# Windowed and dense attention in one encoder layer on one core: meta tokens' keys in a part of their own, and new places on the time line

## The chip, the cores and the metric

The kernel runs on one core of a Trainium2 chip. The metric is device time in microseconds (us), measured from outside. A core has a matrix engine (TensorE, PE in the profile; its weight loads are listed apart as PEld), a vector engine (VectorE, DVE), an activation engine (ScalarE, ACT), a general engine (GpSimd, POOL) and a queue engine that issues transfers (SyncE, SP). Each works through its own instructions in the order in which they stand, and waits on semaphores for the others.

## The reference

One layer, applied to two requests of 1024 tokens each (`g` below) with shared weights. Sixteen meta tokens stand ahead of every request; their rows are dropped from the output. All is float32.

```python
proj = h @ w_in                        # queries, keys, values, z of branches A and B; gates ga, gb
ya = window_attention(rotate(qa), rotate(ka), va, sink) * silu(za)
yb = dense_attention(axial_rope(rms_norm(qb)), axial_rope(rms_norm(kb)), vb) * silu(zb)
merged = sigmoid(ga) * (ya @ w_branch_a) + sigmoid(gb) * (yb @ w_branch_b)
h = layer_norm(ALPHA * h + merged @ w_out)
```

Branch A sees, for a block of 128 queries, the 16 meta keys and the blocks before, at and after its own (|i-j| <= 128), with a sink logit per head. Branch B sees all 16 + 1024 keys. Both have 8 query heads and 2 key-value heads of 64.

## The kernel before

**Precision.** A float32 product is made of three matmuls in the reduced type fp32r: each operand is split into a rounded part (`h`) and a rest (`l`), and the products hh, hl and lh are added in PSUM. So a projection of 128 tokens onto 512 columns is 8 x 3 matmuls of 512 columns. Scores take two matmuls (the query tiles `q1`, `q2` against packed keys), and a value product two (the scores' rounded part `ph` and rest `pl` against values whose rounded part and rest stand side by side).

**Stages.** Stage one (to about 290 us) projects keys and values of all 16 token blocks, and two of the four gates, and keeps keys and values in DRAM (`kd`, `vd`; those of the meta tokens in SBUF tile `mk` and in DRAM `vmd`). Then come branch A (2 requests x 8 blocks), branch B (the same), the other two gates, and a last stage with the branch projections, the output projection and the layer norm. Between A and B lies the handover: `weight_b` (line 840) loads the query and z weights of branch B in 16 pieces of 128 x 512; SP fetches each, ACT rounds it, DVE or POOL makes the rest.

**A unit.** `unit` (line 739) handles one block of 128 queries of one key-value head, four query heads at a time. There are 32 units in each branch. Its steps: `queries` transposes and splits the queries; `scores(h)` makes the scores of head h into one bank of PSUM for each key chunk, and DVE takes minima (in branch A with the mask added); `exps(h)` lets ACT write the exponentials into tiles `p`; `part(k)` takes some keys of all four heads, transposes them on PE (four transposes `st<-ident,p`), copies the result rounded to `ph` on ACT, and subtracts to get `pl` on DVE; `values(k)` adds two 512-wide matmuls, `o<-ph,v` and `o<-pl,v`, to the output bank. `gather`, `scale_z` and `gate` finish the unit.

**Parts.** The meta keys are laid among the others (`keys`, line 608), and `rows` (617) cuts the row of keys in equal parts: in branch A 400 keys into 4 parts of 100 (272 keys into 3 parts of 91, at the first and last block), in branch B 1040 keys into three chunks of 348, 348 and 344, and 9 parts of 116 (the last 112). A 128-row part without meta keys would match the token blocks; here a part takes rows of two blocks, and `chunk` (622) loads values by several transfers, the meta rows by one of them.

**What sets the order.** The functions do not issue instructions but record them. Each recorded step carries a key, a place on a time line (`at`, line 600, with the numbers of `AT`, `LN` and `BOOST`, lines 48 to 51). `Plan.issue` (line 238) then walks all engines in time with a price for every instruction, and at each step lets the engine that is free first take the ready instruction of the lowest key. What comes out is a fixed order for each engine, which the hardware follows. All instructions are recorded at line 279, so rows of the profile differ by tile names only.

Of the kernel before, what the change touches and what calls it, by code (L numbers as in the profile page):

```python
# [12 lines left out]
F32 = mybir.dt.float32  # L13
F32R = mybir.dt.float32r
# [8 lines left out]
P = 128  # L23
# [9 lines left out]
XF = 3  # L33
WF1 = 8
GSPLIT = 1
WB_STEP, WB_LEAD = 1.4, 2.5
DELAY = {
    "pe": {"pe": 0.0, "act": 0.2, "dve": 0.2, "pool": 0.22, "dma": 0.2},
# [3 lines left out]
}  # L42
TABLES = {AF.Exp: "exp", AF.Tanh: "exp", AF.Sigmoid: "sigmoid"}
TABLE_LOAD = 1.28
DMA_ISSUE, DMA_START, DMA_DONE = 0.475, 2.0, 1.8
PB = (7, 3, 3)
KB = 5
BC, BR = 348, 116
NB = 3
OFF = (3, 3)  # L50
ROPE_TAGS = (("rq1", 1), ("rq2", 1), ("rqo", 2))
WSUB = (0, 1, 1, 1)
BOOST = {"rotate": 12, "silu": 12, ("fillq", 0): 2.18, ("fillq", 1): 3.7, ("fillz", 0): -3.9, ("fillz", 1): 4.15, ("values", 0): -1.06, ("values", 1): -1.8, ("gather", 0): 0, ("gather", 1): 0, ("scale_z", 0): 0, ("gate", 0): 0}
LN, LN_LAST = (11.2, 17.85), 18
AT = ({"queries": 22, "scores": 8, "head": 0.7, "exps": 1.85, "part": 2.5},
      {"queries": 22.2, "scores": 6, "head": 4.25, "exps": 4.05, "part": 1.65})
ALPHA = 2.0 ** 0.25
SCALE = HD ** -0.5
NEG = -1e30
# [109 lines left out]
class Plan:  # L169
# [3 lines left out]
    def __init__(self, nc):  # L173
        self.ops, self.rings, self.key = [], {}, 0.0
        self.engines = [Engine(self, e, n) for e, n in
                        ((nc.tensor, "pe"), (nc.scalar, "act"), (nc.vector, "dve"), (nc.gpsimd, "pool"), (nc.sync, "dma"))]
        self.free = {e.id: 0.0 for e in self.engines}
        self.bus, self.tables = 0.0, None

    def tile(self, pool, shape, dtype, tag=None, name=None, bufs=1, space="sbuf"):  # L180
        name = name or tag
# [50 lines left out]
    @staticmethod  # L232
    def delay(d, op):
        if d.eng.id == "dma":
            return DMA_DONE
        return DELAY[d.eng.id][op.eng.id]

    def issue(self):
        done = []
        wait = {e: [] for e in self.free}  # L240
        ready = {e: [] for e in self.free}
        for i, op in enumerate(self.ops):
            op.num = (op.key, i)
            for d in op.deps:
                if d.end is None:
                    d.next.append(op)
                    op.left += 1
                else:
                    op.ready = max(op.ready, d.end + self.delay(d, op))
            if not op.left:  # L250
                heapq.heappush(wait[op.eng.id], (op.ready, op.num))
        for _ in self.ops:
            t, e = min((self.free[e] if ready[e] else max(self.free[e], wait[e][0][0]), e)
                       for e in self.free if ready[e] or wait[e])
            while wait[e] and wait[e][0][0] <= t:
                heapq.heappush(ready[e], heapq.heappop(wait[e])[1])
            op = self.ops[heapq.heappop(ready[e])[1]]
            if op.tables not in (None, self.tables):
                self.tables = op.tables
                t += TABLE_LOAD  # L260
            self.free[e] = op.end = t + op.cost
            if e == "dma":
                self.free[e] = t + DMA_ISSUE
                op.end = self.bus = max(self.bus, t + DMA_START) + op.cost
            for n in op.next:
                n.ready = max(n.ready, op.end + self.delay(op, n))
                n.left -= 1
                if not n.left:
                    heapq.heappush(wait[n.eng.id], (n.ready, n.num))
            done.append(op)  # L270
        for op in done:
# [7 lines left out]
            getattr(op.eng.real, op.name)(*map(real, op.a), **{k: real(v) for k, v in op.k.items()})  # L279
        self.ops = []  # L280


@with_exitstack
def encoder(ctx, tc, d, out):
# [332 lines left out]
    def rows(b, c):  # L617

        n = sum(n for *_, n in keys(b, c))
        return BR if b else -(-n // -(-n // P))  # L620

    def chunk(b, g, e, c):

        if (b, g, e, c) not in chunks:
            at_ = 0
            if e:
                t = kvp.tile([P, 4, NKV, P], F32R, tag="v", name="v", bufs=4)
                r = rows(b, c)
                for meta_, i, m in keys(b, c):
                    while m:  # L630
                        j, o = divmod(at_, r)
                        k, w = (m // r * r, m // r) if o == 0 and m >= r else (min(m, r - o), 1)
                        src = vmd[0:NM, b] if meta_ else vd[b][g]
                        dst = t[o:o + k // w, j:j + w].bitcast(F32)
                        dma(dst, src[i:i + k].rearrange("(w p) v e -> p w v e", w=w))
                        at_, i, m = at_ + k, i + k, m - k
# [10 lines left out]
        return chunks[b, g, e, c]  # L647

    def block_proj(b, g, t, blk, t0, ln):

# [88 lines left out]
    def unit(b, g, t, kvh, blk, t0, ln):  # L739


        cs = list(range(NB)) if b else [t]
        n = [sum(m for *_, m in keys(b, c)) for c in cs]
        r = rows(b, t if b == 0 else 0)
        np_ = [-(-m // r) for m in n]
        parts = [(i, j) for i, m in enumerate(np_) for j in range(m)]
        m0 = 0 if t > 0 else P
        heads = slice(kvh * G, (kvh + 1) * G)
        s = {"p": {}, "part": {}}
# [1 line left out]
        def scores(h):  # L751
# [11 lines left out]
            for i, sx in enumerate(s["sx", h]):  # L763
# [1 line left out]
                if b:  # L765
                    nc.vector.tensor_reduce(out=mn, in_=sx, op=ALU.min, axis=AX.X)
                else:
                    p = s["p"][h, 0] = wk.tile([P, 400], F32, tag=f"p{h if h < 3 else kvh}", name="p", bufs=PB[0])
# [11 lines left out]

        def exps(h):
            for i, sx in enumerate(s["sx", h]):
                if b:
                    s["p"][h, i] = wk.tile([P, 400], F32, tag=f"p{i}", name="p", bufs=PB[0])
                p = s["p"][h, i][:, 0:n[i]]
                act(p, sx if b else p, AF.Exp, scale=-1.0, bias=s["nb"][:, h:h + 1], accum_out=s["rs"][:, h, i:i + 1])

        def sinks():
# [7 lines left out]
                ptt(out=s["rs"][:, :, 0], in0=s["rs"][:, :, 0], in1=s["rs"][:, :, i], op=ALU.add)  # L796

        def part(k):
            i, j = parts[k]
            m = min(r, n[i] - j * r)  # L800
            st = bank("st", 2)[0:m]
            for h in range(G):
                nc.tensor.transpose(st[:, h * P:(h + 1) * P], s["p"][h, i][:, j * r:j * r + m], ident)
            ph = wk.tile([P, 512], F32R, tag="ph", name="ph", bufs=PB[1])[0:m]
            pl = wk.tile([P, 512], F32R, tag="pl", name="pl", bufs=PB[2])[0:m]
            s["part"][k] = ph, pl
            act(ph, st, AF.Copy)
            tt(out=pl, in0=st, in1=ph.bitcast(F32), op=ALU.subtract)

        def values(k):  # L810
            if k == 0:
                s["o"] = bank("o", 1)
            i, j = parts[k]
            m = min(r, n[i] - j * r)
            v = chunk(b, g, 1, cs[i])[0:m, j, kvh]
# [24 lines left out]
    def weight_b(i, t0):  # L840
# [15 lines left out]
        for k in range(KT):  # L856
            at(t0 + WB_STEP * k - WB_LEAD, lambda k=k: fetch(k))
            at(t0 + WB_STEP * k, lambda k=k: piece(k))

    clock, last = 0.0, LN[0]  # L860
    for b in range(2):
        for g in range(2):
            for t in range(NT):
# [172 lines left out]
```

## Time and profile before

| what | value |
|---|---|
| median of 3 runs | 1797.1 us (1795.17 to 1799.28) |
| the profiled execution | 1799.36 us |
| its span, first to last instruction | 1797.6 us |
| busy PE / DVE / ACT / POOL | 1767.0 / 1134.5 / 879.4 / 250.6 us |
| mean granted clock of TensorE | 0.994 |

The span is what the trace covers; the rest of the profiled execution's time lies around it. The profile gives for each group of instructions its tiles as out<-in, its shape (partitions x elements, of a matmul also weights as rows*columns), how often it ran, its busy time in us and the mean duration of one in ns, and then the engine's idle time ahead of it with what ended it. Recorded durations of neighbouring matmuls overlap, since they are pipelined. In the timeline the first number is the start from the beginning of the span, the second the duration; x4 merges four in a row.

### The profile page before, as it was taken

What the parts mean: (1) busy time and instruction counts of PE and PEld (TensorE: products, weight loads), DVE (VectorE), ACT (ScalarE), POOL (GpSimd) and SP (SyncE); (2) the same over time, 40 slices, a digit from 0 to 9 for tenths busy, and PEclk for the clock granted to TensorE, in tenths of its full rate; (3) what the DMA queues carried; (4) which work ended last, traced back from release to release, by engine and by line L of the source; (5) the groups of instructions that cost most, each with busy time, mean ns of one, the idle gap of its engine ahead of it and who ended that gap; (6) DMA issues with size and microseconds to landing.
All of it is one profiled execution on the core that took longest, in us unless ns stands there. A gap on an engine that the chain in (4) does not pass through costs nothing.

```text
span 1797.6 us, 26170 instructions
## 1 busy us (share of the span) xinstructions
PE 1767.0 (98%) x8906; PEld 1453.1 (81%) x8906; DVE 1134.5 (63%) x2900; ACT 879.4 (49%) x2257; POOL 250.6 (14%) x437
## 2 busy tenths in 40 slices
PE   7999999999999999999999999999999999999997
PEld 5787787888888878888888888877888788888886
DVE  6533334777677778888888888886300355555555
ACT  5322223666666677777777777788411310000000
POOL 2000002222221231011111111132000011111110
PEclk9999999999999999999999999999999999999999
DMA  9644445422322340100002000122654643333321
GB/s 326 222 159 143 161 148 161 152 92 91 109 92 91 116 140 32 56 30 34 30 34 77 30 33 30 47 92 68 249 161 152 212 160 117 118 115 115 110 78 48
DMA packets 111083, 199.09 MB, mean 111 GB/s; under 512 B 11796, under 2 KB 49876, under 8 KB 110948
## 3 DMA queue, kind: packets, MB, share of 16 engines
q1 hardware_dynamic: 110948, 197.40, 32.8%
q8 instruction: 71, 1.16, 0.3%
q14 instruction: 64, 0.52, 0.1%
HBM read 138.60 MB, written 58.75 MB: 110 GB/s over the span
## 4 chain that ended last, share of the span: by engine, by line
PE 93%; DVE 2%; DMA 2%; ACT 1%; issue 0%; POOL 0%; SPq 0%; DVEq 0%; ACTq 0%
PE st L279 32%; PE pj L279 26%; PE o L279 18%; PE sx L279 14%; PE tr L279 2%; DMA wf<-in_w_in_dram 0%; DVE mn L279 0%; ACT p L279 0%; DMA gsc<-sg 0%; POOL rope L279 0%; DMA rope<-in_rope_b_dram 0%; DMA wf<-in_wkv_dram 0%; DVE pl L279 0%; SPq L279 0%; DMA sg<-gsc 0%
## 5 line engine op out<-in xcount | busy, mean ns | idle before, releaser
L279 DVE TENSOR_TENSOR pl<-st,ph 116x512 fp32r<-116x512 f32 (+4 forms) x408 | 276.8, 684 | 51.4 <-ACT ph L279 46.1
L279 ACT ACTIVATE ph<-st 116x512 fp32r<-116x512 f32 (+4 forms) x408 | 242.9, 598 | 113.2 <-PE st L279 109.6
L279 PE MATMUL st<-ident,p 128*116 128x128 f32 (+4 forms) x1632 | 257.8, 273 | 3.3 <-ACT p L279 2.2
L279 PE MATMUL sx<-k,q 128*128 128x348 f32 (+3 forms) x1024 | 246.5, 341 | 2.6 <-ACT q L279 0.9
L279 PEld LDWEIGHTS st<-ident,p 128*116 128x116 f32 (+4 forms) x1632 | 198.9, 134 | 52.6 <-issue 7.1
L279 ACT ACTIVATE p<-sx,nb 128x348 f32<-128x348 f32 (+1 forms) x384 | 206.8, 549 | 59.4 <-DVE nb L279 58.7
L279 DVE TENSOR_REDUCE mn<-sx 128x1 f32<-128x348 f32 (+1 forms) x384 | 192.0, 513 | 45.4 <-PE sx L279 42.8
L279 PEld LDWEIGHTS sx<-k,q 128*128 128x128 f32 x1024 | 171.3, 190 | 27.0 <-ACT p L279 4.4
L279 PE MATMUL o<-ph,v 116*128 116x512 f32 (+4 forms) x408 | 176.8, 433 | 0.5 <-DVE yu L279 0.3
L279 DVE TENSOR_TENSOR xl<-xf,xh 128x512 fp32r<-128x512 f32 x64 | 58.2, 927 | 180.6 <-ACT xh L279 180.6
L279 PE MATMUL o<-pl,v 116*128 116x512 f32 (+4 forms) x408 | 164.9, 404 | 1.9 <-DVE pl L279 1.9
L279 ACT ACTIVATE xh<-xf 128x512 fp32r<-128x512 f32 x64 | 38.8, 627 | 258.6 <-PE sx L279 190.1
L279 POOL TENSOR_TENSOR sg<-sg 128x512 f32<-128x512 f32 x32 | 46.9, 1464 | 466.0 <-DVE sg L279 291.8
L279 PE MATMUL pj<-w0h,xh 128*128 128x512 f32 x272 | 111.5, 410 | 0.0
L279 PE MATMUL pj<-w1h,xh 128*128 128x512 f32 x264 | 110.4, 418 | 0.5 <-DVE rope_rq L279 0.5
L279 PE MATMUL pj<-w0h,xl 128*128 128x512 f32 x272 | 108.4, 398 | 0.0
L279 PE MATMUL pj<-w0l,xh 128*128 128x512 f32 x272 | 107.3, 395 | 0.0
L279 PE MATMUL pj<-w1l,xh 128*128 128x512 f32 x264 | 106.2, 402 | 0.0
L279 PE MATMUL pj<-w1h,xl 128*128 128x512 f32 x264 | 105.3, 399 | 0.0
L279 ACT ACTIVATE q<-tr 64x256 fp32r<-64x256 f32 x256 | 96.4, 376 | 16.6 <-PE tr L279 13.8
L279 PEld LDWEIGHTS o<-pl,v 116*128 116x128 f32 (+4 forms) x408 | 77.2, 189 | 20.3 <-DVE pl L279 11.5
L279 ACT ACTIVATE p<-p,nb 128x400 f32<-128x400 f32 (+1 forms) x128 | 75.8, 595 | 33.4 <-DVE nb L279 33.2
(198 smaller groups left out, 3775.0 us busy)
## 6 DMA issues: line engine op xcount, KB each, us to landing
xh<-xsc SPq DMA_DIRECT2D x48, 512.0 KB
xl<-xsc SPq DMA_DIRECT2D x48, 512.0 KB
wf<-in_w_in_dram SPq DMA_DIRECT2D x64, 256.0 KB
gsc<-sg SPq DMA_DIRECT2D x64, 256.0 KB
sg<-gsc SPq DMA_DIRECT2D x64, 256.0 KB
xf<-in_xt_dram SPq DMA_DIRECT2D x32, 256.0 KB
xsc<-xh SPq DMA_DIRECT2D x16, 512.0 KB
xsc<-xl SPq DMA_DIRECT2D x16, 512.0 KB
```

Source lines behind the costliest of these rows:

```text
L279: getattr(op.eng.real, op.name)(*map(real, op.a), **{k: real(v) for k, v in op.k.items()})
```

## The change

Meta keys get a part of their own, and all other keys are cut in parts of 128.

- Branch B's chunks are 384, 384 and 272 keys (the last with the 16 meta keys), with 3 + 3 + 2 parts; branch A has 3 parts (2 in the first and last block). That is one part fewer in each of the 64 units: 344 parts, for 408.
- `meta_near` copies the meta columns of the four heads' exponentials side by side on POOL (`pc`, 128 x 64). `meta_part` transposes them at once on PE, and writes the rounded part into rows 0 to 63 of a tile `pm` (ACT), the rest into rows 64 to 127 (DVE). `meta_out` adds four matmuls `o<-pm,vm`, one for each head, 128 columns wide, with weights `vm` that hold the meta values in that head's rows and zeros elsewhere.
- `vm` is made once for each branch: POOL clears it, and eight transfers of 16 rows fill it.
- The exponentials of the four heads share a tile, with four buffers (two for the third chunk of branch B) for seven of each head's or chunk's; value tiles have 3 slots for 4; weight pieces of the handover use three staging buffers for four.
- The planner assumes 0.9 for 1.8 us as the end of a transfer in stage one. The numbers of the time line are chosen anew (`BOOST`, `LN`, `LN_LAST`, `AT`, and the start of the second weight's load); of these the diff shows two lines.

```diff
-DMA_ISSUE, DMA_START, DMA_DONE = 0.475, 2.0, 1.8
-PB = (7, 3, 3)
+DMA_ISSUE, DMA_START, DMA_DONE = 0.475, 2.0, (0.9, 1.8)
+PB = (4, 2, 3, 3)
-BC, BR = 348, 116
+BC = 384
-AT = ({"queries": 22, "scores": 8, "head": 0.7, "exps": 1.85, "part": 2.5},
+AT = ({"queries": 21.23, "scores": 8, "head": 0.7, "exps": 3.19, "part": 2.0},
...
+    def meta_values(b):
+        t = vm[b] = wk.tile([P, NKV, G, P], F32R, tag="vm", name="vm", bufs=1)
+        nc.gpsimd.memset(t.rearrange("p v h e -> p (v h e)").bitcast(F32), 0.0)
+        for r in (0, 64):
+            for h in range(G):
+                dma(t[r + h * NM:r + (h + 1) * NM, :, h].bitcast(F32), vmd[0:NM, b])
...
         def part(k):
-            i, j = parts[k]
-            m = min(r, n[i] - j * r)
-            st = bank("st", 2)[0:m]
+            i, o = parts[k]
+            st = bank("st", 2)
             for h in range(G):
-                nc.tensor.transpose(st[:, h * P:(h + 1) * P], s["p"][h, i][:, j * r:j * r + m], ident)
+                nc.tensor.transpose(st[:, h * P:(h + 1) * P], s["p"][i][:, h, o:o + P], ident)
...
+        def meta_near():
+            pc = s["pc"] = wk.tile([P, G * NM], F32, tag="pc", name="pc", bufs=2)
+            nc.gpsimd.tensor_copy(pc.rearrange("p (h m) -> p h m", h=G), s["p"][mi][:, :, mo:mo + NM])
+        def meta_part():
+            st = bank("st", 2)
+            nc.tensor.transpose(st[0:64, 0:P], s["pc"], ident)
+            pm = s["pm"] = wk.tile([P, P], F32R, tag="pm", name="pm", bufs=2)
+            act(pm[up], st[0:64, 0:P], AF.Copy)
+            tt(out=pm[dn], in0=st[0:64, 0:P], in1=pm[up].bitcast(F32), op=ALU.subtract)
+        def meta_out():
+            for h in range(G):
+                mm(s["o"][:, h * P:(h + 1) * P], lhsT=vm[b][:, kvh, h], rhs=s["pm"], start=False, stop=False)
...
+        km = META_AT[b]
+        at(t0 + km * slot - T["part"] - 1.5, meta_near, ("part", b))
+        at(t0 + km * slot - T["part"] - 0.01, meta_part, ("part", b))
+        at(t0 + km * slot - 0.01, meta_out, ("values", b))
...
-            f[k] = stage() if k % 4 < 3 else wk.tile([P, 512], F32, tag="wf", name="wf", bufs=1)
+            f[k] = stage()
...
-                    weight_b(1, clock + 2 * ln - 6.53)
+                    weight_b(1, clock + 2 * ln - 8.21)
```

The order of PE in branch A, near the start of the second request. Before (`st<-ident,p` are the transposes of a part, `sx` scores, `o` value products, `tr` transposes of queries and gates, `pj` projections):

```order
L279 MATMUL st<-ident,p 90x128 x4
L279 MATMUL tr<-ident,zr 128x128 x2
L279 MATMUL st<-ident,p 100x128 x4
L279 MATMUL sx<-k,q_5375 128x400
L279 MATMUL sx<-k,q_5189 128x400
L279 MATMUL o<-ph,v 128x512
L279 MATMUL sx<-k,q_5375 128x400
L279 MATMUL sx<-k,q_5189 128x400
L279 MATMUL sx<-k,q_5375 128x400
L279 MATMUL sx<-k,q_5189 128x400
L279 MATMUL o<-pl,v 128x512
L279 MATMUL st<-ident,p 100x128 x4
```

And about the same stretch after, with the transpose of the meta columns (`pc`) and the four narrow matmuls:

```order
L279 MATMUL st<-ident,pc 64x128
L279 MATMUL st<-ident,p 128x128 x4
L279 MATMUL pj<-w0h,xh 128x512
L279 MATMUL pj<-w0l,xh 128x512
L279 MATMUL pj<-w0h,xl 128x512
L279 MATMUL pj<-w0h,xh 128x512
L279 MATMUL pj<-w0l,xh 128x512
L279 MATMUL pj<-w0h,xl 128x512
L279 MATMUL o<-pm,vm 128x128 x4
L279 MATMUL o<-ph,v 128x512
L279 MATMUL o<-pl,v 128x512
L279 MATMUL st<-ident,p 128x128 x4
```

Four transposes of 90, 91 or 100 columns have become four of 128; between the transpose of `pc` and the matmuls that use its split stand four transposes and six projection matmuls. In the handover this distance is once four transposes and three projection matmuls.

The order of POOL in branch B, two units, before (`q` is cleared for later queries, `rs` are the row sums, `zr` the scaled gate):

```order
L279 MEMSET q_9057 64x512
L279 TENSOR_TENSOR rs<-rs 128x4 x2
L279 TENSOR_TENSOR zr<-z,rs 128x256
L279 MEMSET q_9304 64x512
L279 TENSOR_TENSOR rs<-rs 128x4 x2
L279 TENSOR_TENSOR zr<-z,rs 128x256
```

and after:

```order
L279 MEMSET q_7922 64x512
L279 TENSOR_TENSOR rs<-rs 128x4 x2
L279 COPY pc<-p_7787 128x64
L279 TENSOR_TENSOR zr<-z,rs 128x256
L279 MEMSET q_8140 64x512
L279 TENSOR_TENSOR rs<-rs 128x4 x2
L279 COPY pc<-p_8024 128x64
L279 TENSOR_TENSOR zr<-z,rs 128x256
```

The copy of the meta columns has come between the row sums of its unit and the scaling of the gate; the rest stands as it did.

The order of ACT in the handover, where it rounds pieces of the query weights of branch B (`w0h`), before (`p,rs` are exponentials with their sums, `se` the sink's, `ph` the copies of parts):

```order
L279 ACTIVATE w0h<-wf 128x512
L279 ACTIVATE ph<-st 100x512
L279 ACTIVATE p,rs<-p,nb 128x400 x2
L279 ACTIVATE w0h<-wf 128x512 x2
L279 ACTIVATE p,rs<-p,nb 128x400 x2
L279 ACTIVATE se<-se 128x4
L279 ACTIVATE w0h<-wf 128x512
```

and after:

```order
L279 ACTIVATE w0h<-wf 128x512
L279 ACTIVATE ph<-st 128x512
L279 ACTIVATE w0h<-wf 128x512
L279 ACTIVATE p,rs<-p,nb 128x400
L279 ACTIVATE w0h<-wf 128x512
L279 ACTIVATE p,rs<-p,nb 128x400 x2
L279 ACTIVATE z<-pj 128x512
L279 ACTIVATE p,rs<-p,nb 128x400
L279 ACTIVATE w0h<-wf 128x512
```

The two pieces that stood together between the exponentials of two heads each now stand singly, with exponentials and a part's copy between them.

More of the change, by code (lines that the diff above doesn't have):

```diff
@@ L35 @@
 GSPLIT = 1
+META_AT = (1, 6)
 WB_STEP, WB_LEAD = 1.4, 2.5
@@ L52 @@
 WSUB = (0, 1, 1, 1)
-BOOST = {"rotate": 12, "silu": 12, ("fillq", 0): 2.18, ("fillq", 1): 3.7, ("fillz", 0): -3.9, ("fillz", 1): 4.15, ("values", 0): -1.06, ("values", 1): -1.8, ("gather", 0): 0, ("gather", 1): 0, ("scale_z", 0): 0, ("gate", 0): 0}
-LN, LN_LAST = (11.2, 17.85), 18
-AT = ({"queries": 22, "scores": 8, "head": 0.7, "exps": 1.85, "part": 2.5},
-      {"queries": 22.2, "scores": 6, "head": 4.25, "exps": 4.05, "part": 1.65})
+BOOST = {"rotate": 12, "silu": 8.74, ("fillq", 0): 2.18, ("fillq", 1): 8.28, ("fillz", 0): -1.61, ("fillz", 1): 4.65, ("values", 0): -0.49, ("values", 1): -1.8, ("gather", 0): -2.2, ("gather", 1): -1.71, ("scale_z", 0): -2.5, ("gate", 0): 1.57}
+LN, LN_LAST = (11.2, 17.35), 17.68
+AT = ({"queries": 21.23, "scores": 8, "head": 0.7, "exps": 3.19, "part": 2.0},
+      {"queries": 21.21, "scores": 6, "head": 4.22, "exps": 4.18, "part": 1.65})
 ALPHA = 2.0 ** 0.25
@@ L177, in __init__ @@
         self.free = {e.id: 0.0 for e in self.engines}
-        self.bus, self.tables = 0.0, None
+        self.bus, self.tables, self.stage = 0.0, None, 0
     def tile(self, pool, shape, dtype, tag=None, name=None, bufs=1, space="sbuf"):
@@ L230, in price, with delay @@
         return 0.068 + n / (1920 if fast else 960)
-    @staticmethod
-    def delay(d, op):
+    def delay(self, d, op):
         if d.eng.id == "dma":
-            return DMA_DONE
+            return DMA_DONE[self.stage > 0]
         return DELAY[d.eng.id][op.eng.id]
@@ L280, in issue @@
         self.ops = []
+        self.stage += 1
 @with_exitstack
@@ L615, in keys, with parts_of @@
         return [(False, lo * P, (c + 1 - lo) * P), (True, 0, NM)] + [(False, (c + 1) * P, P)] * (hi > c + 1)
-    def rows(b, c):
-        n = sum(n for *_, n in keys(b, c))
-        return BR if b else -(-n // -(-n // P))
+    def parts_of(b, c):
+        parts, meta_at, o = [], None, 0
+        for meta_, _, n in keys(b, c):
+            if meta_:
+                meta_at = o
+            else:
+                parts += range(o, o + n, P)
+            o += n
+        return parts, meta_at, o
     def chunk(b, g, e, c):
@@ L626, in chunk @@
             if e:
-                t = kvp.tile([P, 4, NKV, P], F32R, tag="v", name="v", bufs=4)
-                r = rows(b, c)
+                t = kvp.tile([P, 3, NKV, P], F32R, tag="v", name="v", bufs=4)
                 for meta_, i, m in keys(b, c):
[L630 to L636, printed above, removed]
+                    if not meta_:
+                        w = m // P
+                        dma(t[:, at_:at_ + w].bitcast(F32), vd[b][g][i:i + m].rearrange("(w p) v e -> p w v e", w=w))
+                        at_ += w
             else:
@@ L647, in chunk @@
         return chunks[b, g, e, c]
+    def meta_values(b):
[4 more added lines that the diff above has]
+                dma(t[r + h * NM:r + (h + 1) * NM, :, h].bitcast(F32), vmd[0:NM, b])
+    vm = {}
     def block_proj(b, g, t, blk, t0, ln):
@@ L742, in unit @@
         cs = list(range(NB)) if b else [t]
[L743 to L746, printed above, removed]
+        where = [parts_of(b, c) for c in cs]
+        n = [w[2] for w in where]
+        parts = [(i, o) for i, w in enumerate(where) for o in w[0]]
+        mi, mo = next((i, w[1]) for i, w in enumerate(where) if w[1] is not None)
         m0 = 0 if t > 0 else P
@@ L767, in scores @@
                 else:
-                    p = s["p"][h, 0] = wk.tile([P, 400], F32, tag=f"p{h if h < 3 else kvh}", name="p", bufs=PB[0])
+                    if h == 0:
+                        s["p"][0] = wk.tile([P, G, 400], F32, tag="pp", name="p", bufs=PB[0])
+                    p = s["p"][0][:, h]
                     nc.vector.tensor_tensor_reduce(
@@ L782, in exps @@
             for i, sx in enumerate(s["sx", h]):
-                if b:
-                    s["p"][h, i] = wk.tile([P, 400], F32, tag=f"p{i}", name="p", bufs=PB[0])
-                p = s["p"][h, i][:, 0:n[i]]
+                if b and h == 0:
+                    s["p"][i] = (wk.tile([P, G, 400], F32, tag="pp", name="p", bufs=PB[0]) if i < 2 else
+                                 wk.tile([P, G, 272], F32, tag="p2", name="p2", bufs=PB[1]))
+                p = s["p"][i][:, h, 0:n[i]]
                 act(p, sx if b else p, AF.Exp, scale=-1.0, bias=s["nb"][:, h:h + 1], accum_out=s["rs"][:, h, i:i + 1])
@@ L798, in part @@
         def part(k):
-            i, j = parts[k]
-            m = min(r, n[i] - j * r)
-            st = bank("st", 2)[0:m]
+            i, o = parts[k]
+            st = bank("st", 2)
             for h in range(G):
-                nc.tensor.transpose(st[:, h * P:(h + 1) * P], s["p"][h, i][:, j * r:j * r + m], ident)
-            ph = wk.tile([P, 512], F32R, tag="ph", name="ph", bufs=PB[1])[0:m]
-            pl = wk.tile([P, 512], F32R, tag="pl", name="pl", bufs=PB[2])[0:m]
+                nc.tensor.transpose(st[:, h * P:(h + 1) * P], s["p"][i][:, h, o:o + P], ident)
+            ph = wk.tile([P, 512], F32R, tag="ph", name="ph", bufs=PB[2])
+            pl = wk.tile([P, 512], F32R, tag="pl", name="pl", bufs=PB[3])
             s["part"][k] = ph, pl
@@ L812, in values @@
                 s["o"] = bank("o", 1)
-            i, j = parts[k]
-            m = min(r, n[i] - j * r)
-            v = chunk(b, g, 1, cs[i])[0:m, j, kvh]
+            i, o = parts[k]
+            v = chunk(b, g, 1, cs[i])[:, where[i][0].index(o), kvh]
             for e, p in enumerate(s["part"][k]):
@@ L858, in weight_b @@
             at(t0 + WB_STEP * k, lambda k=k: piece(k))
+    at(-30.0, lambda: meta_values(0))
     clock, last = 0.0, LN[0]
@@ L868, in encoder @@
                     unit(b, g, t, kvh, blk, clock + kvh * ln, ln)
+                if (b, g) == (0, 1) and t == NT - 1:
+                    at(clock + 2 * ln - 0.5, lambda: meta_values(1))
                 if (b, g) == (0, 1) and t == NT - 2:
                     weight_b(0, clock - 2.45)
-                    weight_b(1, clock + 2 * ln - 6.53)
+                    weight_b(1, clock + 2 * ln - 8.21)
                 nb, ng = (b, g + 1) if g == 0 else (b + 1, 0)
```

## The prediction

> **What bounds the kernel now.** I read the page first: the busy shares, and the chain that ended last.
>
> ```profile
> span 1797.6 us, 26170 instructions
> PE 1767.0 (98%) x8906; PEld 1453.1 (81%) x8906; DVE 1134.5 (63%) x2900; ACT 879.4 (49%) x2257; POOL 250.6 (14%) x437
> PE 93%; DVE 2%; DMA 2%; ACT 1%; issue 0%; POOL 0%; SPq 0%; DVEq 0%; ACTq 0%
> ```
>
> TensorE (PE) is busy 98% of the span and carries 93% of the chain. A busy PE need not be full, so next came the table by stretches, for the two attention stages (branch A up to about 610 us, branch B after about 660) and the first 100 us.
>
> ```profile
> 0.00:100.00 100.00, 89.49 (x359) 65.26 (x360) 55.88 (x176) 41.38 (x81) 13.38 (x36) 0.97 0.76 265
> 300.00:610.00 310.00, 309.94 (x1676) 261.14 (x1675) 216.63 (x614) 206.07 (x547) 68.94 (x155) 1.00 0.34 111
> 660.00:1190.00 530.00, 528.70 (x3025) 441.61 (x3025) 462.90 (x1144) 408.74 (x1146) 67.94 (x133) 1.00 0.12 41
> ```
>
> After the stretch and its length stand the busy times of PE, weight loads, DVE, ACT and POOL, then the granted clock. PE has no gaps in either attention stage, and the clock is 1.00. DVE is busy 87% of branch B (462.90 of 530) and ACT 77%: close, not the bound. So a matmul that goes there gives back what one matmul takes from the start of the one before it to its own successor. That pace, not the recorded duration (which overlaps), is what I sum. It is read from the timeline of PE, in branch B:
>
> ```profile
> 1002.43 0.60 PE L279 MATMUL st<-ident,p 128*116 128x128 f32 x4
> 1002.79 0.48 PE L279 MATMUL o<-ph,v 116*128 116x512 f32 x1
> 1003.11 0.48 PE L279 MATMUL sx<-k,q 128*128 128x348 f32 x2
> 1003.43 0.40 PE L279 MATMUL o<-pl,v 116*128 116x512 f32 x1
> 1003.66 0.81 PE L279 MATMUL sx<-k,q 128*128 128x348 f32 x4
> 1004.31 0.60 PE L279 MATMUL st<-ident,p 128*112 128x128 f32 x4
> ```
>
> The first column is the start. One 512-wide matmul takes 1003.66 - 1003.43 = 0.23 us. Four transposes and one such matmul take 1003.11 - 1002.43 = 0.68, so a transpose takes (0.68 - 0.23) / 4 = 0.1125. A 348-wide score takes (1004.31 - 1003.66) / 4 = 0.1625.
>
> **The change part by part.**
>
> *Parts removed.* Each of the 64 units (32 of each branch) has one part fewer: branch B 8 for 9, branch A 3 for 4 (2 for 3 in the end blocks). A part is four transposes and two 512-wide matmuls on PE: 0.68 + 0.23 = 0.91 us. 64 x 0.91 = **58.2 us less**, all on the path, since PE has no gaps there.
>
> *Wider transposes.* The parts that stay load 128 weight columns where 116, 100 or 91 stood. The rows that tell what this costs, and two more widths of the scores:
>
> ```profile
> 310.29 0.67 PE L279 MATMUL sx<-k,q 128*128 128x272 f32 x4
> 310.79 0.40 PE L279 MATMUL pj<-w0h,xh 128*128 128x512 f32 x1
> ...
> 314.84 0.60 PE L279 MATMUL st<-ident,p 128*91 128x128 f32 x4
> 315.19 0.50 PE L279 MATMUL sx<-k,q 128*128 128x272 f32 x2
> 315.53 0.38 PE L279 MATMUL st<-ident,p 128*91 128x128 f32 x2
> ...
> 573.18 0.89 PE L279 MATMUL sx<-k,q 128*128 128x400 f32 x4
> 573.91 0.40 PE L279 MATMUL o<-pl,v 100*128 100x512 f32 x1
> 574.58 0.38 PE L279 MATMUL tr<-ident,rope_rqo 128*128 128x128 f32 x2
> 574.72 0.43 PE L279 MATMUL sx<-k,q 128*128 128x400 f32 x1
> 574.99 0.60 PE L279 MATMUL st<-ident,p 128*100 128x128 f32 x4
> ```
>
> A 272-wide score takes 0.50 / 4 = 0.125, a 400-wide one 0.73 / 4 = 0.1825. Four 91-column transposes and two 272-wide scores take 0.69, so one transpose takes (0.69 - 0.25) / 4 = 0.11. Two 128-column transposes and one 400-wide score take 0.41, so one takes (0.41 - 0.1825) / 2 = 0.114. The columns loaded hardly count: 0.004 us over 37 columns, by which 1024 transposes in B widened by 12 columns and 352 in A by 28 to 37 would cost 2.5 us together. That is below the 0.01 us to which I read starts; I take 0.
>
> The Trainium skill (TensorE: Matmul & The Clock Gate, LDWEIGHTS) has a load time that grows by 1/1.2 ns per column. The load rows here grow less:
>
> ```profile
> L279 PEld LDWEIGHTS tr<-ident,rope_rqo 128*128 128x128 f32 x128 | 16.4, 141 | 1.4 <-issue 0.2
> L279 PEld LDWEIGHTS st<-ident,p 128*90 128x90 f32 x32 | 3.7, 122 | 1.1
> ```
>
> (141 - 122) / 38 = 0.5 ns a column, and behind other work. If the rule set the pace, the estimate from it would be 10 ns more for each of the 1024 and 23 to 31 ns for each of the 352: about 19 us.
>
> *Scores.* 348, 348 and 344 columns become 384, 384 and 272, 1040 both times. By the line through 0.125 (272) and 0.1825 (400), 384 costs 0.175: 0.475 for three, against 3 x 0.1625 = 0.4875. Over 256 such triples in B (32 units, 4 heads, two matmuls each) that is 3 us less at most; the difference is one of rounding, I take 0. Minima and exps handle the same columns in as many pieces: 0.
>
> *Meta part added, on PE.* 64 transposes of 64 columns: 64 x 0.1125 = **7.2 us**. And 256 matmuls, four per unit, whose moving side is 128 wide in fp32r. No such matmul is in this trace. Bounds: the line of the scores, carried on to 128 columns, gives 0.125 - 144 x 0.00045 = 0.060 us. The nearest row above it in width, 272, gives 0.125; it also loads 128 weights in fp32r and streams more. The nearest row in shape, the 128 x 128 transpose, gives 0.1125; I take that one. If width stopped helping, the price is that of the 512-wide one, 0.23. So 256 x 0.1125 = **28.8 us**, between 15.4 and 32.0, and 58.9 at the far end.
>
> The Trainium skill (same page, Back-to-back issue gap) gives 81 ns for a sustained stream of loads and 128-wide matmuls, not said for fp32r. By it the 256 cost an estimated 20.7 us and the sum would be -30.3.
>
> *Meta part on the other engines.* Rows for what goes and for the nearest of what comes:
>
> ```profile
> L279 ACT ACTIVATE ph<-st 116x512 fp32r<-116x512 f32 x256 | 152.9, 600 | 57.7 <-PE st L279 56.6
> L279 ACT ACTIVATE rqsq<-st 128x128 f32<-128x128 f32 x16 | 4.4, 277 | 55.0 <-PE st L279 55.0
> L279 DVE TENSOR_TENSOR pl<-st,ph 116x512 fp32r<-116x512 f32 x256 | 174.0, 684 | 25.5 <-ACT ph L279 22.5
> L279 DVE TENSOR_TENSOR rope_rq<-st,rope 128x128 f32<-128x128 f32 x16 | 4.7, 291 | 50.7 <-ACT rqsq L279 49.4 <-DMA rope<-in_rope_a_dram 1.2
> L279 POOL CAST k<-mk 128x32 fp32r<-128x32 f32 x18 | 3.6, 211 | 7.7 <-PE sx L279 6.9
> L279 POOL TENSOR_TENSOR zr<-z,rs 128x256 f32<-128x256 f32 x64 | 41.3, 645 | 204.5 <-PE tr L279 186.9 <-DVE mn L279 11.8 <-DVE rqa L279 3.3
> ```
>
> Per unit ACT loses a 600 ns copy and gains one of about 277; DVE loses 684 and gains about 291; both get emptier. POOL gains a copy of 64 columns, between 211 and 645 ns, on an engine at 13% in B. It is queued behind the clearing of a query buffer and the row sums, ahead of the scaling of the gate; none of these has PE work due soon. Between the transpose of the meta scores and the first narrow matmul, stand four transposes and six wide matmuls in the order shown of branch A, 4 x 0.1125 + 6 x 0.23 = 1.8 us, and at the tightest place, in the handover, four and three, 1.1 us. They cover an ACT and a DVE step of 0.277 + 0.291 = 0.57 us together. I cost this chain at nothing; without that cover it would be 0.57 us x 64 = 36 us.
>
> *Transfers and buffers.* The meta values come by eight 16-row loads per branch instead of one per chunk (18): about as many. They land long before the first use; the buffer of branch B is reloaded after the last use in A, and used first six slots into B. Weight staging in the handover loses its fourth buffer.
>
> *Places.* What the new order can win or lose is bounded by the waits that are there:
>
> ```profile
> 5.31 0.80 PE L279 MATMUL st<-w2h,xh 128*128 128x512 f32 x1 [5.31 <-ACT w2h L279]
> ...
> 630.61 0.45 PE L279 MATMUL st<-ident,p 128*100 128x128 f32 x1 [2.24 <-ACT p L279]
> 645.77 0.47 PE L279 MATMUL pj<-w1h,xh 128*128 128x512 f32 x1 [0.48 <-DVE rope_rq L279]
> 651.95 0.52 PE L279 MATMUL sx<-k,q 128*128 128x272 f32 x2 [0.88 <-DVE mn L279]
> 658.33 0.74 PE L279 MATMUL sx<-k,q 128*128 128x348 f32 x3 [0.94 <-ACT q L279]
> ```
>
> In the first 100 us PE idles 10.5, of which 5.3 are before its first matmul; the other 5.2 the new order of stage one (planned with shorter landings) can take away or double. The handover idles 2.24 + 0.48 + 0.88 + 0.94 = 4.5. The longest stems from ACT, which stands at a weight piece with exps queued behind it:
>
> ```profile
> 628.66 1.28 ACT L279 ACTIVATE w0h<-wf 128x512 fp32r<-128x512 f32 x2 [2.39 <-DMA wf<-in_w_in_dram]
> ```
>
> The new order on ACT puts exps and copies between single pieces, which speaks for less; three staging buffers speak for more. Both places: 0, between -9.7 and +9.7.
>
> *Sum.* -58.2 + 7.2 + 28.8 = **-22.2 us**. The profiled execution took 1799.36 us (span 1797.6 and 1.8 around it), 2.3 above the median of 1797.1. 1799.4 - 22.2 = 1777.2 there, **1775** as a median. The ends: -58.2 + 7.2 + 32.0 + 9.7 = -9.3 (1788), and with the narrow matmul at 0.1125 and all waits gone -31.9 (1765).
>
> **The rivals.**
>
> *The narrow matmul is paid by its columns* (0.060). Then -58.2 + 7.2 + 15.4 = -35.6: 1761, and 1752 to 1771 with the places. For it: the scores follow a straight line from 400 to 272 columns. Against it: a 128 x 128 transpose does not lie on it. The skill's 81 ns lies between this and my value, at 1767.
>
> *It is paid like a wide one.* Should fp32r lose its pace below some width, the four narrow matmuls cost up to 4 x 0.23 and the meta part 0.92 + 0.1125 = 1.03 us, against 0.91 for the part removed: +0.12 x 64 = +7.9, **1805**. It turns to a loss where one takes over (58.2 - 7.2) / 256 = 0.199 us. For it: no fp32r row under 272 exists here, and a transpose streams 128 columns in the time that the line of the scores gives to 244. Against it: nothing in the rows from 512 to 272 bends.
>
> *Waits take the gain.* The gain makes PE reach ACT's and DVE's results sooner. DVE itself does not become the bound: it loses 0.684 - 0.291 = 0.39 us a unit where PE loses 22.2 / 64 = 0.35. But 0.1 us lost at each narrow group (6.4), the handover's and the start's waits doubled (9.7) give -22.2 + 16.1 = -6: 1791.
>
> *Transposes paid by the weight columns*, the skill's rule above: -22.2 + 19 = -3: 1794. The rows of 91 and 128 columns speak against it.
>
> **How the numbers follow.** The forecast, narrow matmul near 0.11 to 0.125, has 0.50 (its own range 1765 to 1788); by columns 0.20; like a wide one 0.12; waits 0.15; weight columns 0.03. The range 1756 to 1794 takes in the forecast, three quarters of the second, and nearly all of the waits: about 0.8. 0.2%, 3.6 us, is what a measurement of this kernel can tell from no change, so under 1793.5 is faster: 0.50 + 0.20 + 0.12 of the waits = 0.82. Same: the weight columns and the rest of the waits, 0.06. Slower: 0.12.
>
> **What would show it.** Right: 1856 transposes in all for 2048; 688 matmuls o<-ph and o<-pl for 816; four o<-pm,vm that follow each other at 0.10 to 0.125 us; PE still 98% busy; a unit of B shorter by 0.35 us. Wrong: o<-pm at 0.2 or more, gaps of PE released by pm or pc, or a handover that idles 10 us.

## The result and the profile after

The changed kernel takes 1776.3 us (median of 4 runs, 1774.92 to 1777.02) against 1796.1 of the kernel before: a ratio of 0.9889, with a 95% interval of 0.9876 to 0.9901. That is 19.9 us less at a time of 1795; 22.2 was forecast. The profiled execution took 1777.02, its span 1775.2. Below, the difference of two ratios times 1795 us is given as "against the changed kernel" or "against before".

The page after, busy shares and chain:

```profile
span 1775.2 us, 26103 instructions
PE 1739.5 (98%) x8842; PEld 1435.9 (81%) x8842; DVE 1112.9 (63%) x2900; ACT 858.0 (48%) x2257; POOL 263.6 (15%) x503
PE 79%; DVE 13%; ACT 4%; issue 2%; DMA 1%; POOL 1%; SPq 0%; DVEq 0%; POOLq 0%; ACTq 0%
```

TensorE is as full as before (98%), with 64 matmuls fewer. But the chain, 93% TensorE before, now runs 13% through DVE: TensorE meets results that have just become ready. The same two stretches as before, of the attention stages:

```profile
300.00:610.00 310.00, 309.31 (x1675) 259.10 (x1674) 209.41 (x625) 199.62 (x557) 75.34 (x188) 1.00 0.33 113
660.00:1190.00 530.00, 523.38 (x3065) 444.91 (x3064) 464.28 (x1175) 412.84 (x1182) 79.58 (x169) 1.00 0.14 44
```

DVE's share is unchanged (464.28 of 530, 462.90 before). TensorE's idle time in the second went from 1.3 to 6.6 us. Waits that show as idle time are thus a few us; the timeline of TensorE in branch B has the price of the new part:

```profile
756.13 0.38 PE L279 MATMUL st<-ident,p 128*128 128x128 f32 x2
756.27 0.48 PE L279 MATMUL pj<-w0l,xh 128*128 128x512 f32 x1
756.58 0.39 PE L279 MATMUL pj<-w0h,xl 128*128 128x512 f32 x1
756.81 0.56 PE L279 MATMUL o<-pm,vm 128*128 128x128 f32 x4
757.21 0.45 PE L279 MATMUL o<-ph,v 128*128 128x512 f32 x1
757.49 0.39 PE L279 MATMUL o<-pl,v 128*128 128x512 f32 x1
757.72 0.40 PE L279 MATMUL pj<-w0h,xh 128*128 128x512 f32 x1
```

Two transposes of 128 columns and one wide matmul take 756.58 - 756.13 = 0.45, so a transpose takes (0.45 - 0.23) / 2 = 0.11, as the 91-column one did. The four narrow matmuls start at 756.81 and the next at 757.21, 0.40 later. But that next one, 512 wide, takes 757.49 - 757.21 = 0.28, not 0.23: the group also costs its follower 0.05. Group and two wide matmuls take 0.91; less 2 x 0.23, the four cost **0.45 us, 0.1125 each**.

With that, pace alone gives 64 x (-0.91 + 0.1125 + 0.45) = -22.2 us; 19.9 were measured. Pace and waiting are told apart over whole traces at the end of the section on the places.

The steps beside TensorE (duration: least, median, most, ns):

```profile
L279 ACT ACTIVATE pm<-st x64: 252/270/279, 315.4 to 1242.6; 64x128 fp32r<-64x128 f32 x64
L279 DVE TENSOR_TENSOR pm<-st,pm x64: 283/284/286, 317.0 to 1243.5; 64x128 fp32r<-64x128 f32 x64
```

### The profile page after: what moved, and what is told of

The parts are those of the page before. It is cut to its first block, busy times and chain, and to the rows that moved or that the text cites. A ratio compares the mean times of both kernels' runs of the same rounds, so it can differ in the third digit from the quotient of the medians.

```text
span 1775.2 us, 26103 instructions
## 1 busy us (share of the span) xinstructions
PE 1739.5 (98%) x8842; PEld 1435.9 (81%) x8842; DVE 1112.9 (63%) x2900; ACT 858.0 (48%) x2257; POOL 263.6 (15%) x503
## 4 chain that ended last, share of the span: by engine, by line
PE 79%; DVE 13%; ACT 4%; issue 2%; DMA 1%; POOL 1%; SPq 0%; DVEq 0%; POOLq 0%; ACTq 0%
PE st L279 28%; PE pj L279 22%; PE o L279 15%; PE sx L279 11%; DVE mn L279 3%; DVE pl L279 3%; ACT p L279 2%; PE tr L279 2%; DVE rope_rq L279 1%; DVE rqy L279 1%; DVE rqa L279 1%; DVE rqms L279 1%; DVE nb L279 1%; ACT oc L279 1%; DVE rope_rqo L279 1%
## 5 line engine op out<-in xcount | busy, mean ns | idle before, releaser
L279 DVE TENSOR_TENSOR pl<-st,ph 128x512 fp32r<-128x512 f32 x344 | 233.5, 685 | 28.8 <-ACT ph L279 26.1
L279 PE MATMUL sx<-k,q 128*128 128x384 f32 (+2 forms) x1024 | 242.8, 340 | 0.4 <-ACT p L279 0.2
L279 ACT ACTIVATE ph<-st 128x512 fp32r<-128x512 f32 x344 | 204.0, 598 | 78.3 <-PE st L279 75.8
L279 ACT ACTIVATE p<-sx,nb 128x384 f32<-128x384 f32 (+1 forms) x384 | 207.3, 549 | 38.9 <-DVE nb L279 34.0
L279 PE MATMUL st<-ident,p 128*128 128x128 f32 x1376 | 218.8, 273 | 6.6 <-DVE pl L279 5.5
L279 PEld LDWEIGHTS st<-ident,p 128*128 128x128 f32 x1376 | 170.2, 140 | 48.0 <-DVE pl L279 9.2
L279 DVE TENSOR_REDUCE mn<-sx 128x1 f32<-128x384 f32 (+1 forms) x384 | 181.4, 510 | 26.7 <-PE sx L279 25.9
L279 DVE TENSOR_TENSOR xl<-xf,xh 128x512 fp32r<-128x512 f32 x64 | 58.2, 927 | 179.6 <-ACT xh L279 179.6
L279 PE MATMUL o<-ph,v 128*128 128x512 f32 x344 | 154.0, 448 | 1.2 <-DVE yu L279 0.8
L279 PE MATMUL o<-pl,v 128*128 128x512 f32 x344 | 139.4, 405 | 1.5 <-DVE pl L279 1.5
L279 POOL MEMSET q<- 64x512 f32 x64 | 33.3, 521 | 352.0 <-PE sx L279 239.0
```

## The experiments: what sets the price of a narrow matmul

Two theories stood after the result. One: loading 128 weight columns takes about 0.11 us, and a matmul that streams for less than that leaves part of a load in sight. Two: the moving side in fp32r streams slower below some width. Three runs change one size each, with the order of instructions as it was, or the number; one changes where the narrow matmuls stand.

**Twice the number.**

```diff
         def meta_out():
-            for h in range(G):
+            for h in (0, 1, 2, 3, 0, 1, 2, 3):
```

> The four narrow matmuls stand twice, eight in a row (the meta values count twice). If a narrow matmul in a row costs 0.111 us by either theory: 256 x 0.111 = 28 us more, 1805. If it were paid by its columns, 0.06: 15 us more, 1792. If like a wide one, 0.23: 59 us more, 1835.

Measured: 1801.5 us, ratio 1.0032 (1.0021 to 1.0044), 25.7 more than the changed kernel. The timeline of TensorE, in the same place:

```profile
769.17 1.00 PE L279 MATMUL o<-pm,vm 128*128 128x128 f32 x8
770.01 0.45 PE L279 MATMUL o<-ph,v 128*128 128x512 f32 x1
770.30 0.39 PE L279 MATMUL o<-pl,v 128*128 128x512 f32 x1
770.53 0.39 PE L279 MATMUL pj<-w0h,xh 128*128 128x512 f32 x1
```

1.36 - 0.46 = 0.90 for eight, 0.1125 each again. That rules out a price by columns (0.060) and the price of a wide matmul (0.23), which were two rivals of the prediction, and the 0.081 between them. Both theories agree with it. By pace 256 more cost 28.8 us, 3 more than the time shows.

**Half the stream.**

```diff
-                mm(s["o"][:, h * P:(h + 1) * P], lhsT=vm[b][:, kvh, h], rhs=s["pm"], start=False, stop=False)
+                mm(s["o"][:, h * P:h * P + 64], lhsT=vm[b][:, kvh, h], rhs=s["pm"][:, 0:64], start=False, stop=False)
```

> Each narrow matmul streams 64 columns in place of 128 (it leaves out the meta values for half of the queries); same order of instructions. Theory one: the load stays, so three of four keep 0.11 us and only the first of each four gets shorter by some 0.03: 2 us less, 1774. Theory two: half of 0.394 us a unit goes, 64 x 0.197 = 12.6 us less, 1764.

Measured: 1776.7, ratio 0.9891 (0.9876 to 0.9906): no change.

```profile
756.33 0.53 PE L279 MATMUL o<-pm,vm 128*128 128x64 f32 x4
756.69 0.48 PE L279 MATMUL o<-ph,v 128*128 128x512 f32 x1
757.01 0.39 PE L279 MATMUL o<-pl,v 128*128 128x512 f32 x1
757.24 0.39 PE L279 MATMUL pj<-w0h,xh 128*128 128x512 f32 x1
```

The group is 0.04 shorter (0.36) and its follower 0.04 longer (0.32): 0.91 in all, to the hundredth what 128 columns took. Streaming half as much buys nothing, where theory two expected 12.6 us less. Theory two is out. Theory one expected 2 us less, for a shorter first matmul of each group; that one is shorter, but its gain is lost at the follower.

**Half the load.**

```diff
-                mm(s["o"][:, h * P:(h + 1) * P], lhsT=vm[b][:, kvh, h], rhs=s["pm"], start=False, stop=False)
+                mm(s["o"][0:64, h * P:(h + 1) * P], lhsT=vm[b][:, kvh, h, 0:64], rhs=s["pm"], start=False, stop=False)
```

> Each narrow matmul loads 64 weight columns in place of 128 and writes 64 partitions (it leaves out the rests of the meta values); it still streams 128. Theory one: the load halves to about 0.055 us, the stream of 0.058 shows: 64 x 3 x 0.053 = 10 us less, 1766. Theory two: no change, 1776.

Measured: 1771.6, ratio 0.9862 (0.9845 to 0.9878), 4.8 less than the changed kernel.

```profile
753.72 0.40 PE L279 MATMUL o<-pm,vm 128*64 128x128 f32 x4
753.95 0.45 PE L279 MATMUL o<-ph,v 128*128 128x512 f32 x1
754.24 0.39 PE L279 MATMUL o<-pl,v 128*128 128x512 f32 x1
754.47 0.40 PE L279 MATMUL pj<-w0h,xh 128*128 128x512 f32 x1
```

Four take 0.23, and 0.75 - 0.46 = 0.29 with what the follower loses. So a narrow matmul streams its 128 columns in 0.06 us; with 64 weight columns the load is no longer in sight, except for the follower's load of 128. Theory one holds. The edit also halves the partitions that a narrow matmul writes; but the wide matmul is late by 0.06 behind such a one too, while the narrow ones behind it are not, so it is what the next instruction loads that counts. The Trainium skill (TensorE: Matmul & The Clock Gate, LDWEIGHTS) states P / 1.2 ns for a load of P weight columns; an estimate from it is 107 ns for 128 and 53 for 64. The paces of these runs agree, with 0.1125 per load of 128 in sight and at most 0.06 for 64. The recorded durations of the loads themselves are longer, 191 and 135 ns in the median; loads that start 0.11 us apart overlap in the record, as matmuls do. By pace the saving is 64 x (0.45 - 0.29) = 10 us; half of it came back, so that the time alone lies midway between the two theories. This is taken up below.

**Apart from each other.**

```diff
-        def meta_out():
-            for h in range(G):
-                mm(s["o"][:, h * P:(h + 1) * P], lhsT=vm[b][:, kvh, h], rhs=s["pm"], start=False, stop=False)
+        near = ({(km, 0): (0,), (km, 1): (1,), (km + 1, 0): (2,), (km + 1, 1): (3,)} if km + 1 < len(parts) else
+                {(km, 0): (0, 1), (km, 1): (2, 3)})
...
             for e, p in enumerate(s["part"][k]):
+                for h in near.get((k, e), ()):
+                    mm(s["o"][:, h * P:(h + 1) * P], lhsT=vm[b][:, kvh, h], rhs=s["pm"], start=False, stop=False)
                 mm(s["o"], lhsT=v, rhs=p, start=k + e == 0, stop=k + e == len(parts))
...
-        at(t0 + km * slot - 0.01, meta_out, ("values", b))
```

> The four narrow matmuls of a unit are taken apart: each stands alone ahead of one of the wide value products, 224 of 256 singly; nothing else is changed. Theory one (the load of 128 weight columns sets the pace of a narrow matmul, about 0.11 us, unless a wide matmul ahead of it hides the load, when it takes about 0.058): three loads of 0.053 us a unit go out of sight, 64 x 3 x 0.053 = 10 us less than the changed kernel, about 1766 to 1768 us. Theory two (the moving side streams at half the pace below some width, 0.11 us wherever it stands): no change, 1776.

Measured: 1772.4, ratio 0.9871 (0.9856 to 0.9886): 3 less by the ratios, with intervals that overlap. Theory one as it was written expected 10 less, and its mechanism, a wide matmul that hides the load, is not there:

```profile
755.07 0.22 PE L279 MATMUL o<-pm,vm 128*128 128x128 f32 x1
755.13 0.45 PE L279 MATMUL o<-ph,v 128*128 128x512 f32 x1
755.42 0.22 PE L279 MATMUL o<-pm,vm 128*128 128x128 f32 x1
755.48 0.45 PE L279 MATMUL o<-pl,v 128*128 128x512 f32 x1
755.77 0.60 PE L279 MATMUL st<-ident,p 128*128 128x128 f32 x4
```

A narrow matmul alone takes 0.06, its own load hidden behind the wide one ahead, but the wide one behind it takes 0.29 each time. Two narrow ones cost 0.70 - 0.46 = 0.24, 0.12 each: no less than in a row. What a narrow matmul leaves in sight is the load of the *next* instruction, since that load runs beside the narrow stream and outlasts it. A wide matmul ahead does not help with that. The few us that this kernel gained came from less waiting at the same pace (59.1 us for 63.0, in the table below); which waits, these runs don't settle. By its median it is the fastest of the kernels here that compute the whole reference.

## The experiments: what the whole meta part costs

```diff
-        at(t0 + km * slot - T["part"] - 1.5, meta_near, ("part", b))
-        at(t0 + km * slot - T["part"] - 0.01, meta_part, ("part", b))
-        at(t0 + km * slot - 0.01, meta_out, ("values", b))
```

> The meta part is left out altogether (the meta values do not enter; their scores still do): one transpose and four narrow matmuls less on TensorE in each unit, and the copy, rounding and subtraction on the other engines. If every removed microsecond of TensorE comes back: 64 x (0.1125 + 0.394) = 32 us less than the changed kernel, 1742 to 1744. If only about half comes back, as in the run with half the load (4.8 of 10): 16 us less, 1759.

Measured: 1734.0, ratio 0.9656 (0.9643 to 0.9669), 41.8 less than the changed kernel. Pace gives 64 x (0.1125 + 0.45) = 36. So TensorE's time comes back in full here, and about 5 us of waits went with it (57.9 us for 63.0, in the table below). The meta part is thus not quite free beside TensorE; which of its steps costs that, or whether the new order of the rest does, this run doesn't tell. Neither expectation holds: the first counted 32, without the follower's share.

## The experiments: what the new places are worth

**All the old numbers with the new parts, and the reverse.** The first takes BOOST, LN, LN_LAST, AT and the start of the second weight from before into the changed kernel (the diff; its two lines of BOOST stand further down), the second takes the new ones into the kernel before.

```diff
...
-LN, LN_LAST = (11.2, 17.35), 17.68
+LN, LN_LAST = (11.2, 17.85), 18
-AT = ({"queries": 21.23, "scores": 8, "head": 0.7, "exps": 3.19, "part": 2.0},
-      {"queries": 21.21, "scores": 6, "head": 4.22, "exps": 4.18, "part": 1.65})
+AT = ({"queries": 22, "scores": 8, "head": 0.7, "exps": 1.85, "part": 2.5},
+      {"queries": 22.2, "scores": 6, "head": 4.25, "exps": 4.05, "part": 1.65})
...
-                    weight_b(1, clock + 2 * ln - 8.21)
+                    weight_b(1, clock + 2 * ln - 6.53)
```

> The changed kernel with the numbers of the time line from before (boosts, unit lengths, leads, start of the second weight's load). Theory one, the gain is the count of matmuls on TensorE and the places bring little: within 3 us of the changed kernel, 1774 to 1780, ratio 0.989 to 0.991. Rival, the new places bring a good part of the gain: half of it goes, 1785, ratio 0.995.

> The kernel before, with the numbers of the time line of the changed one and nothing else changed. Theory one: no change, within 3 us of before. Rival (new places bring a good part): 8 to 12 us less than before.

Measured: the new parts with the old places 1795.2, ratio 1.0000 (0.9992 to 1.0009); the old parts with the new places 1802.4, ratio 1.0038 (1.0023 to 1.0053). The fewer matmuls with the old numbers bring nothing, the new numbers alone lose 7 us, and both together gain 19.9. The theory that the count of matmuls is the gain and the places bring little has fallen, and by more than its rival said: it expected half of the gain to go. In the kernel before both were wrong, the rival (8 to 12 us less) also in the sign.

Most of where the time goes is seen in branch B. First the stretch from 720 to 1150 us of the changed kernel, then what its weight loads (PEld) waited for there: who, for whom, total us, times, longest.

```profile
720.00:1150.00 430.00, 426.40 (x2509) 364.12 (x2507) 377.56 (x958) 334.64 (x957) 56.41 (x132) 1.00 0.12 40
```

```profile
PEld st L279 <- DVE pl L279: 8.6, 12, 0.7
PEld o L279 <- issue: 5.0, 12, 0.4
```

The same two views of the kernel with the new parts and the old places:

```profile
720.00:1150.00 430.00, 427.78 (x2429) 353.00 (x2429) 366.16 (x921) 319.29 (x927) 55.24 (x128) 1.00 0.11 37
```

```profile
PEld o L279 <- DVE pl L279: 11.1, 34, 0.7
PEld o L279 <- issue: 5.1, 23, 0.3
PEld o L279 <- ACT ph L279: 2.5, 13, 0.2
PEld pj L279 <- issue: 2.5, 12, 0.2
PEld sx L279 <- ACT p L279: 2.1, 12, 0.2
```

TensorE shows the same busy time in both, 426 and 428 of 430 us, yet it ran 2429 matmuls in place of 2509, 3.2% fewer. The waits are 0.1 to 0.7 us each, and most lie under the recorded end of the matmul before. They are seen in the weight loads: `o` waits for DVE's `pl` 34 times with the old places, and not in this list with the new. ACT shows it from the other side, in the group of branch B's exponentials in that stretch; first with the new places, then the old:

```profile
L279 ACT ACTIVATE p<-sx,nb 128x384 f32<-128x384 f32 x191 | 109.5, 578 | 18.8 <-DVE nb L279 14.1
```

```profile
L279 ACT ACTIVATE p<-sx,nb 128x384 f32<-128x384 f32 x186 | 107.1, 580 | 66.3 <-DVE nb L279 65.0
```

ACT stands 65 us for the shifts from DVE where it stood 14. That is a sign, not a size: with the old lengths and leads alone (below) ACT stood 10.6 us for them, and the kernel still lost 6.6. My reading is that with the old places scores, minima, exponentials and parts follow each other with little to spare; the starts of TensorE, summed below, show that matmuls come late at several of these steps.

**Which numbers.** Three runs put back one group each: lengths, leads and the weight's start (the diff above); all of BOOST; or one boost alone.

```diff
-BOOST = {"rotate": 12, "silu": 8.74, ("fillq", 0): 2.18, ("fillq", 1): 8.28, ("fillz", 0): -1.61, ("fillz", 1): 4.65, ("values", 0): -0.49, ("values", 1): -1.8, ("gather", 0): -2.2, ("gather", 1): -1.71, ("scale_z", 0): -2.5, ("gate", 0): 1.57}
+BOOST = {"rotate": 12, "silu": 12, ("fillq", 0): 2.18, ("fillq", 1): 3.7, ("fillz", 0): -3.9, ("fillz", 1): 4.15, ("values", 0): -1.06, ("values", 1): -1.8, ("gather", 0): 0, ("gather", 1): 0, ("scale_z", 0): 0, ("gate", 0): 0}
```

> The changed kernel with the old unit lengths, the old leads of queries, exps and parts, and the old start of the second weight; the new boosts stay. The run with all old numbers lost the whole gain, 19 us. Theory boosts (what stands between parts on TensorE, the query projections above all, decides whether rests come in time): this keeps the gain, 1774 to 1780. Rival leads (scores and exps come too late): most of the 19 us goes, 1788 to 1795.

> The changed kernel with all old boosts; unit lengths and leads stay new. Theory boosts: the gain is lost, 1788 to 1795, with TensorE waiting for pl in branch B. Rival leads: it stays, 1774 to 1780. If each half costs alone and the two do not add: both this and the run with the old leads lie near 1790.

```diff
-BOOST = {... ("fillq", 1): 8.28, ...}
+BOOST = {... ("fillq", 1): 3.7, ...}
```

> The changed kernel with one old number: the boost of branch B's query projections, 3.7 in place of 8.28. If this one decides: 1785 or more, as in the run with all old boosts. If it is one of many: within 4 us of the changed kernel, 1773 to 1780.

Measured: old lengths and leads 1782.2, ratio 0.9926 (0.9909 to 0.9943), 6.6 more than the changed kernel; old boosts 1790.2, ratio 0.9966 (0.9953 to 0.9979), 13.8 more; the one boost of the query projections 1780.3, ratio 0.9913 (0.9898 to 0.9927), 4.3 more. 6.6 + 13.8 = 20.4, against 19.9 for both at once: the two groups add. Boosts weigh more, but neither group nor the one boost decides alone; that boost is about a third of its group. The weight loads' longest waits in the same stretch, first with the old lengths and leads, then with the old boosts:

```profile
PEld o L279 <- DVE pl L279: 11.0, 24, 0.5
PEld sx L279 <- ACT p L279: 8.1, 36, 0.3
```

```profile
PEld o L279 <- DVE pl L279: 15.1, 40, 0.6
PEld sx L279 <- ACT p L279: 6.9, 34, 0.3
```

Either brings the waits for `pl` back, and scores wait for ACT's exponentials, which read the bank that the scores are to be written to. The totals of such lists name who is late, but do not rank the kernels: the first five lines come to 31.0 us with the old lengths and leads, at a loss of 6.6, and to 23.3 with all old numbers, at a loss of 19.9.

**The landing time in stage one.**

```diff
-DMA_ISSUE, DMA_START, DMA_DONE = 0.475, 2.0, (0.9, 1.8)
+DMA_ISSUE, DMA_START, DMA_DONE = 0.475, 2.0, (1.8, 1.8)
```

> The changed kernel with the old assumption of 1.8 us for the end of a transfer in stage one; the later stages keep their order. If the new order of stage one gains what the profiles show up to the first scores (310.3 us before, 308.7 after): 1 to 2 us more than the changed kernel, 1776 to 1779. If that is scatter between executions: no change, 1774 to 1777.

Measured: 1777.4, ratio 0.9896 (0.9881 to 0.9911), within the interval of the changed kernel. Whether it is worth 1 us or nothing stays open.

**A lighter DVE.** If waits for `pl` hold TensorE up, is it DVE that is too slow?

```diff
-            pl = wk.tile([P, 512], F32R, tag="pl", name="pl", bufs=PB[3])
-            s["part"][k] = ph, pl
+            s["part"][k] = ph, ph
             act(ph, st, AF.Copy)
-            tt(out=pl, in0=st, in1=ph.bitcast(F32), op=ALU.subtract)
```

> The rest pl of every part is left out: VectorE makes no subtraction of 0.685 us for 344 parts (235 us less on VectorE), and TensorE multiplies ph twice instead, so its work is the same. The order is planned anew with it. If TensorE alone bounds both attention stages: within 4 us of the changed kernel, 1773 to 1777. If results of VectorE that come late keep part of a saving from showing: 10 us less or more, 1766 or below.

Measured: 1776.7, ratio 0.9894 (0.9881 to 0.9907): no change, as expected for a kernel that TensorE alone bounds, with DVE at 64% of branch B's stretch in place of 88%:

```profile
720.00:1150.00 430.00, 427.42 (x2503) 361.87 (x2502) 275.49 (x768) 329.40 (x952) 56.03 (x132) 1.00 0.12 40
```

```profile
PEld sx L279 <- ACT p L279: 10.9, 24, 0.7
```

The waits have moved to the scores, and 2503 matmuls run where 2509 did. So in the changed kernel DVE's load is not what costs. That it is the distance in the order between a step and the step that uses it, at whichever step it is shortest, fits this but was not shown: no run has the lighter DVE with the old places.

**Pace and waiting apart.** The time from each matmul's start to the next one's can be summed over a whole trace. As the pace of a step I take the lower quartile, over the fourteen traces, of all steps with the same shapes of the matmul, the one ahead and the one behind; what a step takes beyond it is counted as waiting, seen as idle time or not. In us:

| kernel | pace | waiting |
|---|---|---|
| before | 1718.8 | 63.4 |
| changed | 1696.6 | 63.0 |
| narrow matmuls twice | 1724.5 | 59.9 |
| half the stream | 1696.7 | 62.9 |
| half the load | 1688.0 | 67.1 |
| apart from each other | 1696.2 | 59.1 |
| no meta part | 1658.8 | 57.9 |
| new parts, old places | 1696.8 | 83.5 |
| old parts, new places | 1720.2 | 64.3 |
| old lengths and leads | 1695.4 | 68.6 |
| old boosts | 1694.4 | 80.0 |
| one old boost | 1696.5 | 67.1 |
| no rests | 1694.6 | 65.1 |

With the lowest tenth or the median as the pace, the split shifts by 6 to 11 us, nearly alike in all kernels; the differences to the changed kernel move by at most some 2 us. The change took 22.2 us of pace and left the waiting as it was. (The profiled execution of the kernel before was 3.2 us above its median, that of the changed one 0.7; this is where the 2 us between 22.2 and the 19.9 measured lie.) The old places leave the pace alone and add 20.5 us of waiting, 14.6 of it in branch B and 4.6 in branch A and the handover; it rose most ahead of the matmuls with `pl` (6.3 to 15.6) and of the scores (6.3 to 15.8). And the halved load has its missing half here: 8.6 us less pace, 4.1 more waiting.

## Why the prediction came out right, and where it was wrong

- *Parts removed*, 58.2 us, and *wider transposes* at nothing: right. A 128-column transpose takes 0.11 us after the change. The rule by loaded columns, which would have made the transposes 19 us dearer, does not set their pace. "No gaps", on which the first term rested, was read from busy times; by its starts the kernel before waited some 63 us, as the changed one did. The term holds because the waiting stayed the same.
- *The narrow matmul* at 0.1125, taken from the transpose as the row nearest in shape: right to the hundredth, by another cause, and so by luck. The transpose has that pace whatever it loads; the narrow matmul has it by the load of the next weights. That the two numbers meet is nothing that these runs explain. So the rule that the trace spoke against for transposes is the one that prices the narrow matmuls.
- *The rivals by columns* (0.060) and *like a wide one* (0.23) are ruled out by the doubled group. 0.06 is the narrow stream, and it shows only where the loads are halved.
- *DVE not the bound*: right for the changed kernel, shown by the run without the rests.
- *The chain of the meta part at nothing*: off by about 5 of the 41.8 us that the run without the meta part saves.
- *Places: 0, between -9.7 and +9.7*: the 0 came out, the working failed. I bounded it by the idle times on TensorE's timeline, in the start and the handover. What the places decide lies mostly in branch B, in waits of tenths of a us that the timeline counts as busy. Given the new parts, the new numbers are worth 19.9 us, twice my bound; without them the whole gain is lost, which is the rival *waits take the gain*, only in another place and larger. The sum held because the change brings the numbers that keep the waiting at what it was (63.0 us for 63.4), and I had assumed that they stay so without asking what would keep them there.

## What to carry to other kernels

On a full matrix engine, sum a change by start-to-start pace, with its follower's delay included; a matmul whose stream is shorter than the next weight load costs that load. In a kernel whose order comes from a planner's numbers, a saving of instructions is only as good as the order that is made for it: test the new code with the old numbers before the gain is put down to the code. Waits under the recorded end of a matmul don't show as idle time; sum the starts, or count matmuls in equal stretches, for the size, and read the weight loads' waits for who is late.

## What the runs showed of the hardware

- A matmul of 128 columns in fp32r streams in 0.06 us; in a row of such matmuls, each with a load of 128 weight columns, one takes 0.1125; a load of 64 does not show beside 0.06. (The loads are recorded with 191 and 135 ns.) The part of a load that outlasts the stream of the matmul ahead of it delays the instruction that it belongs to: the wide matmul behind a narrow one took 0.28 to 0.29 us in place of 0.23, and 0.32 when the narrow one streamed 64 columns.
- Transposes of float32 took 0.11 us with 91 as with 128 weight columns.
